# RMSNorm with Swish on one core: gamma brought to all 128 partitions by its own broadcast transfer

## The chip, the core and the metric

One core of a Trainium2 chip runs the kernel. In the profiles DVE is the vector engine, ACT the scalar engine and POOL the GpSimd engine; SP and ACT issue transfers (SPq and ACTq in the views), and 16 DMA engines, called transfer engines here, carry them in packets, each of which is one record of the profile. The time is the device time of one execution, in microseconds; three to nine executions of a kernel are quoted as a median with their lowest and highest. Kernels compared here were run in turn on the same chip, and each is compared with runs of the kernel before from the same rounds.

## The reference

`x` is 16 x 1024 x 512 float32 (16,384 rows of 512, 33.55 MB), `gamma` has 512 numbers, all 1.0 in this input.

```python
rms = np.sqrt(np.mean(x ** 2, axis=-1, keepdims=True) + eps)
x_norm = x / rms * gamma
out = x_norm * (1.0 / (1.0 + np.exp(-x_norm)))
```

So every row is read once and written once, 67.1 MB in all, with some arithmetic between.

## The kernel before

The rows pass through a ring of 96 rows per partition. A tile is 8 rows per partition (the first two are 4), one transfer each way; arithmetic goes in chunks of 4 rows. Loads are issued on the SP queue, stores and gamma on the ACT queue. gamma goes to four partitions (0, 32, 64, 96) of a zeroed tile, and a shuffle on DVE copies the first partition of each group of 32 to the rest.

```python
sizes = [4, 4] + [8] * 15        # rows per partition of each tile
ring, ahead, cn, n_act = 96, 32, 4, 3
...
gamma4 = pool.tile([P, D], fp32, name="gamma4")
gamma_sb = pool.tile([P, D], fp32, name="gamma_sb")
...
def norm(k):
    for j in range(cn):
        row = xb[:, chunks[k] + j, :]
        nc.vector.scalar_tensor_tensor(
            out=row, in0=row, scalar=rstd[:, k, j : j + 1],
            in1=gamma_sb[:], op0=ALU.mult, op1=ALU.mult,
        )
...
    nc.gpsimd.memset(gamma4[:], 0.0)
    nc.gpsimd.memset(neg_half[:], -0.5)
    nc.scalar.dma_start(out=gamma4[0:P:32, :], in_=gamma.partition_broadcast(4))
    nc.scalar.preload_act_table_set("silu_and_others")

    # ... the loads of the first 32 rows are issued here ...
    for k in range(K + 3):
        if k < K:
            sums(k)          # squares: 3 rows on ACT, 1 on DVE
            root(k)          # 1/rms on DVE and POOL
        while stored < len(tiles) and ends[stored] <= k - 2:
            store(stored)
            stored += 1
        if k == 0:
            nc.vector.stream_shuffle(gamma_sb[:], gamma4[:], [0] * 32)
        if 1 <= k <= K:
            norm(k - 1)
        if 2 <= k < K + 2:
            swish(k - 2)     # ACT
            # ... issue the next loads ...
```

## Time and profile before

| | before |
|---|---|
| time, median of the first 3 runs | 164.03 us (163.86 to 164.15) |
| span of the profiled run | 162.1 us |
| DVE, ACT, POOL busy | 68%, 73%, 29% |
| moved | 67.15 MB, 414 GB/s over the whole span |

From the profile page of the kernel before: the DMA and GB/s rows cut the span into 40 slices (a digit is the busy share of the 16 transfer engines in tenths; GB/s is what they moved). Then the two queues (q1 carries the loads; q10 the stores and gamma), and from the page's list of groups the two instructions that the change takes away: line, engine, operation, output and input, count, then busy us and mean ns of one, then the idle time before it.

```profile
DMA  4999999999999999999999999999999999999992
GB/s 162 439 437 449 392 376 423 437 429 419 433 425 441 429 425 437 433 425 437 433 425 437 433 425 433 437 425 433 435 414 445 429 421 441 429 425 441 429 425 121
DMA packets 4908, 67.15 MB, mean 414 GB/s; under 512 B 548, under 2 KB 548, under 8 KB 552
...
q1 hardware_dynamic: 2448, 33.56, 49.3%
q10 hardware_dynamic: 2456, 33.56, 48.4%
...
L140 DVE STREAM_SHUFFLE gamma_sb<-gamma 128x512 f32<-128x512 f32 x1 | 0.7, 724 | 0.0
L114 POOL MEMSET gamma<- 128x512 f32 x1 | 0.5, 525 | 0.3 <-POOLq L164 0.3
```

The transfer engines are busy from the second slice to the last but one, so the kernel is bound by them: what lengthens their work lengthened the run (2.02 us of added packets cost 2.24 us, m3_mid below), and less arithmetic did not shorten it (0.7 us of shuffle taken from DVE, 0.03 us, n1_none below).

The beginning in the timeline of the kernel before: start in us, duration in us, engine, line, operation; in brackets how long the engine sat idle and what ended that.

```profile
0.73 0.53 POOL L114 MEMSET gamma<- 128x512 f32 x1 [0.29 <-POOLq L164]
0.74 6.03 SPq L70 DMA_DIRECT2D xb<-in_x_dram  x7
1.29 1.09 ACTq L116 DMA_DIRECT2D gamma<-in_gamma_dram  x1
5.59 0.63 ACT L80 ACTIVATE junk_a<-xb 128x512 bf16<-128x512 f32 x1 [1.90 <-DMA xb<-in_x_dram]
7.68 0.72 DVE L140 STREAM_SHUFFLE gamma_sb<-gamma 128x512 f32<-128x512 f32 x1
8.11 0.63 ACT L80 ACTIVATE junk_a<-xb 128x512 bf16<-128x512 f32 x1 [0.57 <-DMA xb<-in_x_dram]
10.17 2.07 DVE L104 SCALAR_TENSOR_TENSOR xb<-xb,rstd,gamma_sb 128x512 f32<-128x512 f32 x3
```

Load 0 is there at 5.59 us (ACT's first squares), load 1 at about 8.11, and the shuffle's output is first read at 10.17.

### The profile page before, as it was taken

How to read it: one execution, taken by the hardware profiler on the slowest of the kernel's cores; microseconds unless marked ns; L12 is line 12 of the kernel's file. 1: busy time of each engine (PE TensorE's matmuls, PEld its weight loads, DVE VectorE, ACT ScalarE, POOL GpSimd, SP SyncE). 2: the span in 40 equal slices, each digit the busy share in tenths (PEclk: the TensorE clock that was granted, in tenths of full speed). 3: DMA queues.
4: the chain of work that ended last, by engine and by line, in shares of the span. 5: the costliest groups of instructions: out<-in, count | busy, mean ns of one | idle time of the engine just before them, and what ended most of it. 6: DMA issues, size and time to landing. Idle time of an engine off the chain costs nothing.

```text
span 162.1 us, 629 instructions
## 1 busy us (share of the span) xinstructions
DVE 110.3 (68%) x226; ACT 118.8 (73%) x225; POOL 46.4 (29%) x38
## 2 busy tenths in 40 slices
DVE  0376999998996800970088978859998999998000
ACT  3447999999996009800799889499999999996300
POOL 1052433333441300330033423333333444430000
DMA  4999999999999999999999999999999999999992
GB/s 162 439 437 449 392 376 423 437 429 419 433 425 441 429 425 437 433 425 437 433 425 437 433 425 433 437 425 433 435 414 445 429 421 441 429 425 441 429 425 121
DMA packets 4908, 67.15 MB, mean 414 GB/s; under 512 B 548, under 2 KB 548, under 8 KB 552
## 3 DMA queue, kind: packets, MB, share of 16 engines
q1 hardware_dynamic: 2448, 33.56, 49.3%
q10 hardware_dynamic: 2456, 33.56, 48.4%
q14 instruction: 4, 0.03, 0.0%
HBM read 33.56 MB, written 33.55 MB: 414 GB/s over the span
## 4 chain that ended last, share of the span: by engine, by line
DMA 47%; ACT 36%; issue 4%; DVE 3%; another core or an unknown queue 1%; SPq 0%; ACTq 0%; DVEq 0%
DMA xb<-in_x_dram 36%; ACT junk_a L80 19%; ACT xb L111 17%; DMA out_dram<-xb 12%; DVE xb L104 3%; SPq L70 0%; ACTq L73 0%; DVEq L178 0%; DVE aeps L93 0%; ACTq L80 0%
## 5 line engine op out<-in xcount | busy, mean ns | idle before, releaser
L104 DVE SCALAR_TENSOR_TENSOR xb<-xb,rstd,gamma_sb 128x512 f32<-128x512 f32 x128 | 87.4, 745 | 0.0
L111 ACT ACTIVATE xb<-xb 128x2048 f32<-128x2048 f32 x32 | 60.7, 1897 | 23.1 <-DMA xb<-in_x_dram 21.2
L97 POOL TENSOR_TENSOR rstd<-aeps,neg_half 128x4 f32<-128x4 f32 x32 | 45.6, 1426 | 98.5 <-DVE aeps L93 98.5
L80 ACT ACTIVATE junk_a<-xb 128x512 bf16<-128x512 f32 x96 | 58.9, 615 | 6.9 <-DMA xb<-in_x_dram 6.9
L93 DVE TENSOR_SCALAR aeps<-ms 128x4 f32<-128x4 f32 x32 | 5.4, 170 | 32.8 <-ACT junk_a L80 32.8
L86 DVE CUSTOM_DVE_ANT_0 junk_v<-xb 128x512 bf16<-128x512 f32 x32 | 21.9, 683 | 6.0 <-DMA xb<-in_x_dram 6.0
L80 ACT ACTIVATION_READ_ACCUMULATOR junk_a<-xb 128x1 f32 x96 | 18.0, 187 | 0.0
L117 ACT ACT_TABLE_LOAD x1 | 1.3, 1283 | 2.4 <-issue 2.4
L86 DVE DVE_READ_ACCUMULATOR2_ANT ms<- 128x1 f32 x32 | 2.6, 81 | 0.0
L140 DVE STREAM_SHUFFLE gamma_sb<-gamma 128x512 f32<-128x512 f32 x1 | 0.7, 724 | 0.0
L114 POOL MEMSET gamma<- 128x512 f32 x1 | 0.5, 525 | 0.3 <-POOLq L164 0.3
L164 POOL MEMSET const-float32-0.0<- 128x1 f32 x1 | 0.1, 99 | 0.2 <-issue 0.2
L115 POOL MEMSET neg_half<- 128x4 f32 x1 | 0.1, 103 | 0.0
L164 POOL MEMSET const-bfloat16-1.0<- 128x1 bf16 x1 | 0.1, 102 | 0.0
L164 POOL MEMSET const-uint8-127<- 128x1 uint8 x1 | 0.1, 102 | 0.0
L164 POOL MEMSET const-float32-1.0<- 128x1 f32 x1 | 0.1, 99 | 0.0
L140 DVE LOAD_MASK_SELECT gamma_sb<-gamma x1 | 0.0, 14 | 0.0
## 6 DMA issues: line engine op xcount, KB each, us to landing
xb<-in_x_dram SPq DMA_DIRECT2D x15, 2048.0 KB, 44.0
out_dram<-xb ACTq DMA_DIRECT2D x15, 2048.0 KB, 17.5
xb<-in_x_dram SPq DMA_DIRECT2D x2, 1024.0 KB, 5.8
out_dram<-xb ACTq DMA_DIRECT2D x2, 1024.0 KB, 14.5
gamma<-in_gamma_dram ACTq DMA_DIRECT2D x1, 8.0 KB
```

The source lines that it names most:

```text
L80: nc.scalar.activation(out=junk[:], in_=row, func=AF.Square, accum_out=ms[:, k, j : j + 1],)
L86: nc.vector.tensor_tensor_reduce(out=junk[:], in0=row, in1=row, scale=1.0, scalar=0.0, op0=ALU.mult, op1=ALU.add, accum_out=ms[:, k, j : j ...
L93: nc.vector.tensor_scalar(out=aeps[:, k, :], in0=ms[:, k, :], scalar1=inv_d, scalar2=eps_f, op0=ALU.mult, op1=ALU.add,)
L97: nc.gpsimd.tensor_tensor(out=rstd[:, k, :], in0=aeps[:, k, :], in1=neg_half[:], op=ALU.pow)
L104: nc.vector.scalar_tensor_tensor(out=row, in0=row, scalar=rstd[:, k, j : j + 1], in1=gamma_sb[:], op0=ALU.mult, op1=ALU.mult,)
L111: nc.scalar.activation(out=rows, in_=rows, func=AF.Silu)
L114: nc.gpsimd.memset(gamma4[:], 0.0)
L115: nc.gpsimd.memset(neg_half[:], -0.5)
L117: nc.scalar.preload_act_table_set("silu_and_others")
L140: nc.vector.stream_shuffle(gamma_sb[:], gamma4[:], [0] * 32)
L164: nc = _bacc.Bacc("TRN2", target_bir_lowering=False, num_devices=1)
```

## The change

The intent: one transfer fills gamma's 128 partitions by itself, so the zeroed tile, the wait of gamma's transfer for POOL, and the shuffle on DVE go away.

```diff
-    gamma4 = pool.tile([P, D], fp32, name="gamma4")
     gamma_sb = pool.tile([P, D], fp32, name="gamma_sb")
...
-        nc.gpsimd.memset(gamma4[:], 0.0)
         nc.gpsimd.memset(neg_half[:], -0.5)
-        nc.scalar.dma_start(out=gamma4[0:P:32, :], in_=gamma.partition_broadcast(4))
+        nc.scalar.dma_start(out=gamma_sb[:], in_=gamma.partition_broadcast(P))
...
-            if k == 0:
-                nc.vector.stream_shuffle(gamma_sb[:], gamma4[:], [0] * 32)
```

## The prediction

> **What bounds the kernel now.** The transfers. In the page's 40 slices the DMA row reads 9 from the second slice to the last but one; for 3 to 158 us the DMA view gives 66.41 MB at 428 GB/s with the 16 engines about 100% busy (q1 50.9%, q10 49.9%). DVE (68%) and ACT (73%) have slack. The last store is issued at 151.2 us and lands 9.9 us later, behind stores already queued: the transfer backlog finishes last, not the arithmetic. The chain of waits names ACT for 36%, but only feeding a queue that never runs dry.
>
> **What the change removes.**
> - POOL: the 128x512 memset, 0.53 us at 0.73. ACT's gamma transfer waited for it (issued 1.29 us), so it can go out some 0.5 us earlier, about when the first load does (0.74).
> - DVE: the shuffle, 0.72 us at 7.68. The first normalisation, at 10.17, waits for the second tile's sums, which ACT (waiting for a load until 8.11) ends at about 10.0. So DVE waits anyway. Worth 0.
> - 4 gamma packets of 2 KB.
>
> **What it adds.** 128 packets of 2 KB, 0.26 MB, on the same engines. The trace's gamma packets took about 84 ns each (q10 between 5.4 and 5.8 us: three packets are 7.9% of 16 engines' 0.2 us). Estimate: 128 x 84 ns / 16 = 0.67 us of every engine. [...] the trace agrees for 4 (548 packets under 512 B are 34 x 16 + 4 completions).
>
> **What moves.** Loads, stores and their waits keep their order. The first normalisation waits for gamma's transfer itself. Before, gamma landed at 6.44 us (the load queue's 2.5 us wait for it), its packets being served once load 0 was nearly through. I expect 6 to 7.5 us now, still before 10.17. The first or second load lands about 0.6 us later; ACT's first squares shift by up to that, which later slack absorbs.
>
> **On the critical path.** The engines are full from 3 us to the end, so added packets lengthen the span about one for one: +0.65 us. A little may hide in the ramp (engines only 60% busy in the first 5 us). Against that stands a risk I can't cost from this trace: all 16 engines read the same 2 KB of HBM 128 times. [...] I weigh that in: +0.8 us.
>
> **Prediction: 164.8 us, 8 times in 10 between 164.2 and 166.0.** Faster by over 2%: 0.01. Within 2%: 0.95. Slower by over 2%: 0.04.
>
> **What would show each step.** q10 with 124 more data packets and 0.25 MB more; gamma's mean packet time near 84 ns (right) [...]. Gamma landed before 10 us, no DVE wait on it. Later stretches at about 428 GB/s, the last store landed about 0.6 us later. POOL and DVE busy down 0.5 and 0.7 us with no gain in span.
>
> **What would make it wrong.** Gamma packets much slower than 84 ns; gamma served only after several loads, past 10 us; a ramp that hides all of it; or a changed interleaving of loads and stores worth half a microsecond either way.

The sum of the forecast is 0.65 us for the added packets and about 0.15 us for the repeated read, +0.8 us in all, so 164.8 us. "The trace agrees for 4": the transfer of 4 rows ended in 4 completion packets. The division by 16 and the 0.15 us stand as estimates of mine.

## More of the kernel before

Stretches of the run in the windows view of the kernel before: the stretch in us, its length, busy us (and instructions) of DVE, ACT and POOL, the clock, the busy share of the transfer engines, and GB/s.

```profile
0.00:10.00 10.00, 2.12 (x7) 5.12 (x13) 1.78 (x7) 1.00 0.84 335
10.00:16.00 6.00, 4.53 (x10) 3.06 (x8) 2.21 (x2) 1.00 0.96 412
16.00:24.00 8.00, 7.57 (x16) 8.00 (x16) 3.55 (x3) 1.00 1.02 396
24.00:32.00 8.00, 7.57 (x16) 8.00 (x18) 2.88 (x2) 1.00 1.00 423
32.00:155.00 123.00, 88.56 (x180) 94.59 (x175) 35.98 (x25) 1.00 1.01 431
```

From 16 to 24 us the engines are as busy as ever (1.02) and move less (396 GB/s against 431 later): the 16 KB packets that start there take 685 ns on average, those after 32 us 612 ns.

## The result, and the profile after

| | before | after |
|---|---|---|
| time, median | 164.03 us (163.86 to 164.15) | 164.78 us (164.69 to 164.88) |
| span of the profiled run | 162.1 us | 163.1 us |

The ratio is 1.0047, with a 95% interval of 1.0029 to 1.0064: 0.5% slower, inside "within 2%". A ratio is the mean time of one kernel's fast runs over that of the other's of the same rounds, so not quite the ratio of the medians that are quoted.

The same lines of the page of the changed kernel:

```profile
DMA  5999999999999999999999999999999999999992
GB/s 152 339 450 426 430 426 434 424 442 420 434 430 434 426 430 442 422 430 434 426 434 430 438 426 430 434 430 434 424 432 426 430 442 418 430 442 422 434 430 96
DMA packets 5044, 67.41 MB, mean 413 GB/s; under 512 B 560, under 2 KB 560, under 8 KB 688
...
q1 hardware_dynamic: 2448, 33.56, 48.9%
q10 hardware_dynamic: 2592, 33.82, 48.7%
```

q10 has 136 packets more, 124 of data (128 of gamma for 4) and 12 of completion. From the completions I infer how many engines took part (the records do not name the engine): 548 small packets were 34 transfers x 16 + 4, and 560 are 34 x 16 + 16, so 4 engines for the 4 rows and 16 for the 128 rows.

But the picture in the slices is not that of a little more work. The second slice fell from 439 to 339 GB/s, and the fifth and sixth rose from 392 and 376 to 430 and 426. The timeline of the changed kernel at the beginning:

```profile
0.73 0.41 ACTq L114 DMA_DIRECT2D gamma_sb<-in_gamma_dram  x1
0.74 6.87 SPq L69 DMA_DIRECT2D xb<-in_x_dram  x7
7.29 0.63 ACT L79 ACTIVATE junk_a<-xb 128x512 bf16<-128x512 f32 x1 [4.84 <-DMA xb<-in_x_dram]
9.94 0.63 ACT L79 ACTIVATE junk_a<-xb 128x512 bf16<-128x512 f32 x1 [0.70 <-DMA xb<-in_x_dram]
12.01 1.41 DVE L103 SCALAR_TENSOR_TENSOR xb<-xb,rstd,gamma_sb 128x512 f32<-128x512 f32 x2
```

And its stretches in the windows view:

```profile
0.00:10.00 10.00, 1.00 (x4) 3.29 (x8) 0.72 (x6) 1.00 0.83 285
10.00:16.00 6.00, 4.10 (x9) 3.06 (x10) 2.06 (x2) 1.00 1.01 434
16.00:24.00 8.00, 6.84 (x14) 8.00 (x19) 2.88 (x2) 1.00 1.00 428
24.00:32.00 8.00, 7.49 (x16) 8.00 (x16) 3.28 (x3) 1.00 0.99 422
32.00:155.00 123.00, 90.34 (x183) 96.41 (x178) 37.01 (x26) 1.00 1.01 431
```

The first squares start 1.70 us later (7.29 for 5.59), the second tile's 1.83 us later. In the first 10 us 2.85 MB were moved instead of 3.35 MB (285 and 335 GB/s times 10 us), though 0.25 MB more were asked for. Then, from 16 to 24 us, 428 GB/s instead of 396: that stretch gives about 0.6 us back (32 GB/s x 8 us = 0.26 MB, at 431 GB/s). From 32 us on both run at 431. So a loss of some 1.6 us and a gain of some 0.8 us make the 0.75 us. The predicted number was right; of these two terms the predicted sum had the loss only as a risk, weighed in at about 0.15 us (0.65 made 0.8), and the gain not at all.

### The profile page after: what moved, and what is told of

Same layout as the page of the kernel before. It is cut to its first block, busy times and chain, and to the rows that moved or that the text cites. A ratio compares the mean times of both kernels' runs of the same rounds, so it can differ in the third digit from the quotient of the medians.

```text
span 163.1 us, 627 instructions
## 1 busy us (share of the span) xinstructions
DVE 109.8 (67%) x224; ACT 118.8 (73%) x225; POOL 45.9 (28%) x37
## 4 chain that ended last, share of the span: by engine, by line
DMA 48%; ACT 35%; issue 5%; DVE 3%; another core or an unknown queue 1%; SPq 0%; ACTq 0%; DVEq 0%
DMA xb<-in_x_dram 37%; ACT junk_a L79 19%; ACT xb L110 16%; DMA out_dram<-xb 11%; DVE xb L103 3%; SPq L69 0%; ACTq L72 0%; DVEq L174 0%; DVE aeps L92 0%; ACTq L79 0%
```

## The experiments

Two measures are worked out from the packet records of each trace. **Load 3 landed**: each load ends in 16 completion packets, as many as there are engines; their mean time for load 3, about 17 us, tells how much later the loads are once the beginning is over. **Slow time**: over all packets that start between 12 and 45 us, the time above the usual one (611 ns for 16 KB, 309 for 8 KB, 84 for 2 KB, the medians in the kernel before), added up and divided by 16 engines. For the kernel before these are 17.27 us and 0.92 us; for the changed kernel 18.88 and 0.07. Each kernel has one kept trace, and all are set against the one of the kernel before. With the difference of the medians beside them, for all kernels whose gamma traffic is at the start:

| kernel | read by the gamma-like transfer | time against before, us | load 3 later by, us | slow time less by, us | difference of the two |
|---|---|---|---|---|---|
| n1_none | nothing | -0.03 | -0.12 | -0.02 | -0.10 |
| q2_apart | 128 different pieces of 512 B | +0.05 | +0.34 | 0.12 | +0.21 |
| d1_distinct | 128 different rows of 2 KB | +0.47 | +0.60 | 0.21 | +0.39 |
| d2_again | the same | +0.40 | +0.62 | 0.33 | +0.29 |
| q1_quarter | one piece of 512 B, 128 times | +0.65 | +1.67 | 0.87 | +0.80 |
| changed kernel | one row of 2 KB, 128 times | +0.75 | +1.61 | 0.85 | +0.76 |
| a2_again | the same | +0.89 | +1.75 | 0.86 | +0.89 |
| w1_wait | the same, 0.6 us later | +0.67 | +1.68 | 0.86 | +0.82 |
| s1_behind | the same, on the load queue | +0.84 | +1.76 | 0.86 | +0.90 |
| r1_row | row 0 of x, 128 times | +0.75 | +1.51 | 0.85 | +0.66 |
| b3_start | gamma 384 times | +2.12 | +2.73 | 0.63 | +2.11 |

The last column, "later by" minus "slow time less by", comes within 0.16 us of the measured time in every row.

### First four: is it the bytes?

Theory A was the prediction's: each added packet costs its own time on full engines, 128 x 84 ns / 16 = 0.67 us. These four ran on one chip; before took 163.90 us there (163.83 to 164.05, 9 runs).

**n1_none** takes gamma's transfer away altogether.

```diff
-        nc.scalar.dma_start(out=gamma_sb[:], in_=gamma.partition_broadcast(P))
+        nc.gpsimd.memset(gamma_sb[:], 1.0)
```

> gamma (all ones in this input) is written into gamma_sb by a memset, so no gamma transfer at all; the result stays right. Theory A (bytes on full transfer engines: each added 2 KB packet costs its own time): within 0.1 us of the kernel before, 163.9 to 164.1, because 4 packets are 0.02 us of 16 engines and the memset and the shuffle of before lay off the path. Rival R (the shuffle or the memset of before was worth something, so the changed kernel saved it back and its transfer costs more than 0.7 us): over 0.3 us faster than before.

Measured: 163.87 us (163.75 to 163.89), ratio 0.9994 (0.9981 to 1.0008). Rival R falls: the shuffle, the small transfer and its wait for POOL cost nothing that can be measured. (POOL still does a memset of the same size here, so the 0.5 us of the memset itself is not taken away.) It is also the limit for any cleverer way to bring gamma in: 0.03 us by the medians, and by the interval no more than 0.3 us.

**d1_distinct** keeps the changed kernel's transfer but lets it read different rows.

```diff
-        nc.scalar.dma_start(out=gamma_sb[:], in_=gamma.partition_broadcast(P))
+        nc.gpsimd.memset(gamma_sb[:], 1.0)
+        nc.scalar.dma_start(out=scratch[:], in_=xf[0:P, :])
```

> As n1_none, plus the changed kernel's transfer in its place, but from 128 different 2 KB rows of x into a scratch tile: same bytes, packets, engines and moment, no repeated source. Theory A: +0.65 to +0.8 us on before, as the changed kernel, and the packets as slow (about 117 ns mean). Rival C (the repeated read of one 2 KB piece of HBM is a hot spot): packets back to 84 ns and +0.3 to +0.5 us only.

Measured: 164.37 us (164.35 to 164.45), ratio 1.0029 (1.0016 to 1.0041), +0.47 us; the packets' mean was 92 ns against the changed kernel's 117. This was rival C's number, the first sign against A, though the interval overlapped that of the changed kernel, which had run elsewhere.

**b3_start** makes the broadcast three times as wide.

```diff
-    gamma_sb = pool.tile([P, D], fp32, name="gamma_sb")
+    gamma_w = pool.tile([P, 3, D], fp32, name="gamma_w")
...
-        nc.scalar.dma_start(out=gamma_sb[:], in_=gamma.partition_broadcast(P))
+        for_all = gamma.partition_broadcast(P)
+        nc.scalar.dma_start(
+            out=gamma_w[:], in_=for_all.unsqueeze(1).to_broadcast([P, 3, D])
+        )
```

> The changed kernel with its broadcast three times as wide (384 packets of 2 KB, 768 KB, one transfer at the start, a third of it used). Theory A: 3 x 0.67 to 3 x 0.75 = +2.0 to +2.25 us on before. Rival B (a fixed cost of disturbing the first loads, whatever the bytes): +0.8 to +1.2. Rival C (hot spot): over +2.7.

Measured: 166.02 us (165.98 to 166.16), ratio 1.0130 (1.0116 to 1.0143), +2.12 us, in the middle of A's range.

**m3_mid** leaves the gamma path of before and adds the same 384 packets at chunk 12.

```diff
+            if k == 12:
+                for_all = gamma.partition_broadcast(P)
+                nc.scalar.dma_start(
+                    out=scratch[:],
+                    in_=for_all.unsqueeze(1).to_broadcast([P, 3, D]),
+                )
```

> The kernel before, with its own gamma path, plus the same 384 broadcast packets into a scratch tile in the middle of the run (chunk 12). Theory A: the same as b3_start within 0.3 us, +2.0 to +2.25 on before. Rival B (the cost comes from the start: later first load, later first store): under +0.5, if the middle has slack; if the engines are full there too but the start has an extra cost, m3_mid is clearly below b3_start.

Measured: 166.14 us (166.07 to 166.76; the highest is the profiled run), ratio 1.0144 (1.0128 to 1.0159), +2.24 us. Its gamma packets are served from 74.5 to 91.5 us, each in 84 ns, which makes 384 x 84 / 16 = 2.02 us. In the full middle of the run, where these reads are spread over 17 us, A holds: the added packets cost about their own time (2.24 us for 2.02).

After this round A looked confirmed three times, with one dissenter. The dissenter was right.

### Second four: the repeat, the moment, or the queue?

On one chip; before took 164.01 us (163.85 to 164.14, 9 runs).

**a2_again** is the changed kernel and **d2_again** is d1_distinct, both without an edit.

> The changed kernel unedited, on the chip of the next three, for its interval and a second trace. Theory A: +0.65 to +0.85 us on before. In its first trace 0.25 us of that was gamma packets slower than 84 ns and first loads slower than their usual 309 ns a packet; if that is real and not a draw, gamma's mean packet is again over 105 ns.

> d1_distinct unedited (memset gamma, same transfer from 128 different rows of x), beside the changed kernel on one chip. Theory A (bytes alone): equal to a2_again within 0.1 us. Rival C' (the repeated source is slow in the start alone, for both queues): 0.2 to 0.4 us below a2_again, gamma-sized packets near 90 ns, first loads near their usual 309 to 340 ns.

Measured: a2_again 164.90 us (164.82 to 164.98), ratio 1.0056 (1.0043 to 1.0068); d2_again 164.41 us (164.24 to 164.58), ratio 1.0025 (1.0013 to 1.0038). The two do not overlap: on one chip, at one moment, with the same bytes, packets and engines, reading one row 128 times costs 0.49 us more than reading 128 rows. gamma's packets took 134 ns on average, the different rows' 84. Theory C' stands, and the bytes explain only about half.

**w1_wait** puts the old issue time back.

```diff
+        nc.gpsimd.memset(gamma_sb[:], 0.0)
         nc.scalar.dma_start(out=gamma_sb[:], in_=gamma.partition_broadcast(P))
```

> The changed kernel with a memset of gamma_sb ahead of its transfer, so that the transfer waits for POOL and is issued at about 1.3 us as before's was, not at 0.73. Theory A: as a2_again within 0.1 us. Rival D (going out together with load 0[...] is what costs the extra): 0.2 to 0.4 us below a2_again, near +0.5 on before, and load 0 lands near 5.6 to 6.2 us instead of 7.3.

Measured: 164.68 us (164.47 to 164.77), ratio 1.0039 (1.0027 to 1.0052). The transfer was issued at 1.32 us and load 0 did land early, as D expected (first squares at 5.65 us), but load 1 landed as late as in a2_again (9.53 and 9.56 us by the completion packets, against 7.68 before). The loss only moved from load 0 to load 1. Its 0.22 us below a2_again is too little to tell (the intervals overlap), so D may hold a small part, and not the bulk.

**s1_behind** moves gamma to the load queue, behind loads 0 and 1.

```diff
-        nc.scalar.dma_start(out=gamma_sb[:], in_=gamma.partition_broadcast(P))
...
             loaded += 1
+            if loaded == 2:
+                nc.sync.dma_start(
+                    out=gamma_sb[:], in_=gamma.partition_broadcast(P)
+                )
```

> The changed kernel with gamma's broadcast moved to the load queue, behind loads 0 and 1, so that it interleaves with nothing; 128 packets as before it. Theory A: +0.6 to +0.75 us, as a2_again within 0.1, although the first squares start at 5.6 us as in the kernel before. Rivals C' and D: 0.2 to 0.4 us below a2_again. Rival B (the later first load is what costs): at before, +0.1 at most.

Measured: 164.85 us (164.71 to 164.91), ratio 1.0053 (1.0039 to 1.0066), as a2_again. Rival B falls: the first squares start at 5.61 us as before and the time is that of the changed kernel. D falls as the main cause. My line for C' ("0.2 to 0.4 us below") was wrong as well: I had taken the slowness for one of two queues colliding. Here gamma collides with nothing, and its reads are at their slowest, 206 ns a packet on average. The DMA view of s1_behind from 7.5 to 9.5 us, in 40 slices of 0.05 us:

```profile
DMA  2979949999039993339997039997039997997999
GB/s 82 492 287 451 451 123 205 164 164 164 0 41 205 164 164 41 41 41 164 205 164 82 0 41 164 205 164 82 0 41 533 369 533 328 697 1024 328 369 656 656
```

The engines read as busy nearly throughout, at a fraction of their rate until 9.0 us, when the next load takes over. gamma's 0.262 MB took from 7.48 to 9.54 us (start of its first packet to its last completion), 127 GB/s. The queue made no difference here: 164.85 us with gamma on the load queue, 164.90 with it on ACT's (a2_again).

### Last four: the size, the source, and the slow loads at 16 to 24 us

In the windows view, the kernels that had one place read repeatedly at the start lost 1.6 us and lacked the slow stretch; those that hadn't kept it. Three kernels on one chip (before 164.07 us, 163.83 to 164.38, 9 runs), the fourth in a later session on another chip (before 163.99 us, 163.91 to 164.14, 9 runs).

**r1_row** repeats another source.

```diff
-        nc.scalar.dma_start(out=scratch[:], in_=xf[0:P, :])
+        nc.scalar.dma_start(out=scratch[:], in_=xf[0, :].partition_broadcast(P))
```

> d1_distinct with one edit: the 128 packets read row 0 of x 128 times, not 128 different rows; gamma by memset. Theory H (a row read by all 16 engines is slow while they read it together): as the changed kernel and not as d1_distinct: packets over 105 ns on average, load 0 landing near 7.0 us, +0.75 to +0.95 us on before, and no slow loads at 18 to 23 us. Rival (something of gamma's own tensor or the draw of runs): as d1_distinct, +0.4 to +0.5.

Measured: 164.82 us (164.77 to 164.93), ratio 1.0048 (1.0035 to 1.0060), and no slow loads. It is the repeat, not gamma's own tensor. One line of the expectation missed: the packets' mean was 91 ns, not over 105. The lost time need not stand in the durations of the repeated packets; here it stood partly in gaps (the engines' busy share in the first 10 us was 0.76, against 0.84 before).

**q1_quarter** repeats with a quarter of the bytes.

```diff
-        nc.scalar.dma_start(out=gamma_sb[:], in_=gamma.partition_broadcast(P))
+        nc.gpsimd.memset(gamma_sb[:], 1.0)
+        nc.scalar.dma_start(
+            out=scratch[:, 0:128], in_=gamma[0:128].partition_broadcast(P)
+        )
```

> gamma by memset; the broadcast transfer reduced to the first 128 numbers of gamma, 128 packets of 512 B into a scratch tile, so a quarter of the bytes with the same number of reads of one place. Theory A and H: 0.2 to 0.3 us on before if the slow loads at 18 to 23 us stay (they cost the kernel before 0.76 us of every engine). Rival E (a repeated read at the start shifts the engines so that those slow loads don't happen): they vanish and the kernel is 0.3 to 0.5 us faster than before.

Measured: 164.72 us (164.69 to 164.87), ratio 1.0045 (1.0031 to 1.0058), +0.65 us. Theory A falls here: 64 KB cost nearly as much as 256 KB. Load 3 came 1.67 us later. Rival E was half right, and only that half: the slow loads did vanish, but they did not pay for the start.

**q2_apart** reads as little, from different rows.

```diff
-            out=scratch[:, 0:128], in_=gamma[0:128].partition_broadcast(P)
+            out=scratch[:, 0:128], in_=xf[0:P, 0:128]
```

> q1_quarter with one edit: the 128 packets of 512 B come from 128 different rows of x, not 128 times from gamma. q1_quarter cost +0.65 us with a quarter of the bytes, so bytes alone are no longer the explanation of the changed kernel's time. Theory H (the repeat is what costs, by the number of reads of one place and not by bytes): load 1 lands within 0.4 us of before's 7.7 us (q1_quarter's landed at 9.7), 0.0 to +0.25 us on before. Rival N (the number of packets costs, whatever their source and size): as q1_quarter, +0.55 us or more.

Measured: 164.04 us (163.99 to 164.18), ratio 1.0003 (0.9990 to 1.0017), +0.05 us. Load 1 landed at 8.19 us, against 7.68 before and 9.70 in q1_quarter, so 0.5 us rather than within 0.4, but rival N is out: 128 packets of 512 B cost next to nothing when each reads another place. With q1_quarter, this is the pair that settles it: the two ran on different chips, but each beside the kernel before, and the intervals of their ratios do not meet. The windows view of q1_quarter:

```profile
0.00:10.00 10.00, 0.87 (x3) 3.23 (x7) 0.85 (x7) 1.00 0.79 262
...
16.00:24.00 8.00, 6.79 (x14) 8.00 (x17) 2.88 (x2) 1.00 1.00 430
```

and of q2_apart, the same stretches:

```profile
0.00:10.00 10.00, 1.57 (x5) 4.62 (x12) 1.77 (x7) 1.00 0.84 321
...
16.00:24.00 8.00, 7.57 (x16) 8.00 (x15) 3.60 (x3) 1.00 0.99 383
```

Same bytes, 59 GB/s apart in the first 10 us (0.59 MB, 1.4 us at 431 GB/s); and 47 GB/s the other way from 16 to 24 us (0.38 MB, 0.9 us).

The packet records say where the loss at the start stands. The repeated packets of q1_quarter were no slower than the different ones of q2_apart: 27 ns on average in both. But the 256 packets of 8 KB of the first two loads took 411 ns on average against 356 ns, which is 0.88 us of each of the 16 engines, and between 2.5 and 9.5 us the engines stood idle for 0.5 us in q1_quarter and not at all in q2_apart. So here the loads beside the repeated reads are held up; in s1_behind, with nothing beside them, it was the repeated packets themselves. Their mean time alone is no measure of the loss.

The words "by the number of reads" in the expectation go too far. b3_start made three times as many reads of the same 2 KB and its load 3 was 2.73 us later, of which 2.02 are its packets' own time at 84 ns: its extra was 0.7 us, less than the changed kernel's 0.9 (1.61 less 0.67), not three times it. m3_mid had no slow gamma packets at all (84 to 89 ns). What is shown is that 128 reads of one place within a few microseconds at the start (by 16 engines, going by the completions) put load 3 back by 0.9 to 1.3 us more than the same bytes from 128 places (2 KB and 512 B pieces); how it grows with their number is not.

**t1_later** asks what the slow stretch of the kernel before hangs on.

```diff
-        for k in range(K + 3):
+        for k in range(K + 5):
-            while stored < len(tiles) and ends[stored] <= k - 2:
+            while stored < len(tiles) and ends[stored] <= k - 4:
```

> The kernel before with each store issued two chunks later (and the loop two longer). It tells what the slow loads at 18 to 23 us of the kernel before hang on. If on the first stores (20.5 us): they move with them to about 26 us or later. If on the loads' place in x: they stay at 18 to 23 us. Time: within 0.5 us of before, as the engines stay full.

Measured: 163.81 us (163.78 to 163.98), ratio 0.9987 (0.9975 to 1.0000): the same. Its windows view:

```profile
16.00:24.00 8.00, 7.56 (x16) 8.00 (x15) 3.60 (x3) 1.00 1.01 432
24.00:32.00 8.00, 7.57 (x16) 8.00 (x18) 3.00 (x3) 1.00 0.99 386
```

Before had 396 and 423 in these rows. The slow stretch moved from 16-24 us to 24-32 us with the first stores (first store packet at 26.54 us here, 20.46 before), so it goes with the beginning of the stores and not with a place in x. It does not wait for the stores' data, though: the first slow load packets start at 23.9 us here and 18.5 us before, after the first store is issued (22.43 and 16.78 us) and some 2 us or more ahead of its first packet. (For the kernel before, about 0.4 of its 0.92 us stand ahead of that packet; here about 0.6 of 0.88.)

**Left open.** Why the slow stretch is missing after a repeated read at the start is not known. It was absent in all six traces of the five kernels that made 128 such reads there (slow time 0.05 to 0.07 us), reduced in b3_start, and present in the seven other traces, but no run shows the mechanism. Nor did any run delay the start by the same 1.6 us without a repeated read, so it may be the delay that removes the slow stretch and not the repeat: with different places read, a load 3 later by 0.34 us (q2_apart) and 0.6 us (d1_distinct, d2_again) went with a slow time of 0.80, 0.71 and 0.59 us, each below the 0.92 of before. It is open, too, what makes the repeated read slow. No version beat both kernels clearly: n1_none and t1_later lie within the noise of before. n1_none bounds what gamma's path alone can give; the 0.92 us of the slow stretch is more than that, but no run kept the early start of the kernel before and lost the stretch.

## Why the prediction was right, and where not

- **The time**: 164.8 predicted, 164.78 measured, in a range of 164.2 to 166.0. Right.
- **What bounds the kernel**: the transfers. Right; the removal of the shuffle's 0.7 us of DVE work, of the small transfer and of its wait for POOL gained nothing (n1_none, 0.03 us).
- **"DVE waits anyway. Worth 0"**, said of the shuffle: right by the same run.
- **The step that failed: "added packets lengthen the span about one for one: +0.65 us", at "about 84 ns each".** gamma's packets took 117 and 134 ns on average in the two traces, the first loads' packets beside them 387 and 376 ns against 338 before, and bytes are not what the transfer cost: a quarter of them cost +0.65 us (q1_quarter), a quarter without the repeat +0.05 (q2_apart), all of them without the repeat +0.40 to +0.47. In the place of one term of +0.65 stand a loss of 1.6 us at the start and 0.85 us given back around the first stores. That these nearly make the same number was luck.
- **The 84 ns itself** came from four packets, which ended in four completions. It was a fair price for a packet (84 to 89 ns in m3_mid, 84 on average in d2_again) and said nothing of 128 reads of one place together.
- **The risk was named, and it was the real one**: "all 16 engines read the same 2 KB of HBM 128 times". The repeated read measured alone on its queue took 2.06 us (127 GB/s, s1_behind). It entered the sum with about 0.15 us only.
- **"The first or second load lands about 0.6 us later"**: 1.7 us. **"which later slack absorbs"**: right for ACT and DVE (73% and 67% busy); the transfers have none (a busy share of 1.01 from 32 to 155 us).
- **gamma lands between 6 and 7.5 us, before it is needed**: right, 6.7 us after its issue at 0.73, and no wait on it.
- **"Later stretches at about 428 GB/s"**: the number is right (428 from 16 to 24 us, 431 after 32 us), but the line took the kernel before to run at that rate too, and from 16 to 24 us it ran at 396. I had seen the dip of before in the slices and did not ask what it was.

## What to carry to other kernels

At the start of this kernel a broadcast transfer was not priced by its bytes (a quarter of them cost 0.65 us for 0.75 to 0.89), though in the middle, spread over 17 us, it was (m3_mid, 2.24 us for 2.02). Where all engines fetch the same few bytes at once, price the repeat by a run; in a kernel bound by transfers, few copies from memory and the spreading on an engine with slack, as in the kernel before, were worth 0.75 us here. When an experiment scales a suspected cause, scale it down too and swap the source: three times the bytes agreed with the wrong theory, a quarter of the bytes refuted it. And a total that comes out right is not yet a confirmed sum; look in the slices for a loss and a gain that cancel.
